# Preparing the output weights of a hybrid attention and recurrence block: half beside the input projection, half beside attention's own projection

## The chip, the core and the metric

The kernel runs on one core of a Trainium2 chip. A core has a matrix engine (TensorE, PE in the profile; its weight loads are PEld), a vector engine (VectorE, DVE), an engine for functions and copies (ScalarE, ACT), a general engine (GpSimd, POOL) and one that only issues transfers (SyncE, SP). Each runs its own instructions in order and waits for the others on semaphores. Transfers between HBM, the large memory, and SBUF, the memory on the chip, are issued by SP, ACT or POOL and carried out by 16 DMA engines. Matmuls write into PSUM, eight banks of 512 float columns.

The metric is the time of one execution in microseconds (us) of device time. A profile is one execution with a record of every instruction: its span runs from the first instruction to the last.

## The reference

One layer of a decoder on a sequence of 1024 tokens of width 1024, in float32. The input is normalised and modulated by a condition `c`, one wide projection makes the inputs of two branches (attention with a window of 128 and a learned sink for each head; a gated linear recurrence), both branches are projected, merged by sigmoid gates, projected again, scaled by a gate made of `c`, added to the input and normalised.

```python
mod = c @ w_ada[l] + b_ada[l]
shift, scale, gate = jnp.split(mod, 3, axis=-1)
h = rmsnorm(x, norm_g[l]) * (1.0 + scale[:, None, :]) + shift[:, None, :]
proj = h @ w_in[l]
q, k, v, g_attn, xr, g_rnn, m_attn, m_rnn = jnp.split(proj, SPLIT_POINTS, axis=-1)
...
denom = jnp.sum(p, axis=-1, keepdims=True) + jnp.exp(sink - m)
...
merged = (jax.nn.sigmoid(m_attn) * (y_attn @ w_attn_proj[l])
          + jax.nn.sigmoid(m_rnn) * (y_rnn @ w_rnn_proj[l]))
x = x + gate[:, None, :] * (merged @ w_out[l])
...
return rmsnorm(x, final_g)
```

Two things of it matter here. `gate * (merged @ w_out)` is computed as `merged @ (w_out * gate)`: the gate row is made from `w_ada`, and the columns of `w_out` are multiplied by it once. And the sinks, 16 numbers, take part in every maximum of attention's scores.

## The kernel before

**Numbers.** A float32 operand is used as a sum of two reduced-precision parts, a high part (`wh`, `hh`, `nh`, ...: a cast on ACT) and the remainder (`wl`, `hl`, `nl`, ...: a subtraction on DVE). Each product is three matmuls: high by high, low by high, high by low. `cast` (L103) and `rest` (L109, and L111 where the weights are scaled) make the two parts of a weight tile.

**The order of the stages.** First the input is normalised and turned, and the first columns are projected (to about 91 us). Then comes the main part of the input projection, on TensorE lines L708 and L1021 (to about 597 us); attention runs from 567 to 745 us amid the end of the projection and the recurrence's projection (`rp_steps`, L171); then attention's projection (`ap_k`, L171, to 838.5 us); then the output projection (`gemm`, L1853) with the last normalisation. Up to L1747 the order on all engines is the program's own (`manual_schedule`); from there to L1924 a planner of the compiler orders the instructions of every engine; from L1925 (`last`) PE, ACT and DVE are again in the program's order.

**The input projection.** `pairs` lists 23 pairs of column chunks. A pair is seven products of 12 matmuls each (a scheme that needs seven products of half-size blocks in place of eight, with sums of weight blocks made by DVE in `tsum`, L730). One product is a slot of about 2.75 us; there are 161 products, numbered by `W["slot"]` in `run`. The first of a product's matmuls needs the high part of its weights, the second the low part, which is made one slot ahead. Beside the products there are four sorts of work on ACT and DVE: what a slot must do (`fixed`), the recurrence's steps (`waiting[0]`, `waiting[1]`), its gate products (`extra`, L1021, 5.5 us each), and work that is due only at the very end (`idle`).

**How `idle` is paced.** `Load.pe`, `Load.act` and `Load.dve` are a running estimate of when each engine will be through with what it has been given. After each slot, `background` first gives out the recurrence's steps as far as the estimate of ACT or DVE does not exceed the end of the slot by more than 2.8 or 2.2 us, then up to four entries of `idle`, as far as it does not exceed it by `slack`. `slack` is 1.0 up to slot 55, then 1.3, or -1.0 while both lists of the recurrence hold work. An entry of `idle` is a list of steps, or a condition that must hold before the next is given out (`slots(n)`: n slots later).

**What is in `idle`.** `w_out_gate` (L1183): eight tiles of `w_gate` (128 x 1024) are loaded by SP into two buffers `wr`, scaled on DVE by their value of `c` and summed in `gate_bc` (L1195, L1198); the sum over the partitions is a product with ones (L1221), which leaves the gate row on every partition (L1227). Then `w_out_blocks(k)` (L1238) for k = 0 to 3: two tiles of `w_out` are loaded, multiplied by the gate row on DVE (`scale`, L1248, 128 x 1024), combined by four differences of halves (`diff`, L1257, 128 x 512), and seven results of 128 x 512 are stored to HBM (`wo_d[0]` to `wo_d[6]`). The output projection loads those back (`load_b`, L1762) and splits them (L1768, L1769).

**Attention's start.** `open_attn` (L1275) opens attention's buffers once the recurrence's lists are empty, and issues the first loads: keys and queries on SP (`load_kq`), the sinks and the values on POOL. It is followed by the units `u` = 0 to 31: `scores` (TensorE, L1325), `maxima_a` (ACT copies scores, L1334), `maxima_d` (for the first block of a group a mask on POOL, L1343; then the negated maximum on DVE, L1345), `weights_a` (exponentials on ACT, L1350), and so on, with one product of the projection between the units (`piece`). `sink(u)` (L1310) copies the sinks into the tile over which the maximum runs, on POOL (L1313).

**The end.** The last row of tiles (row 7) is computed in two halves of 256 columns: `add_to` adds to the input on DVE (L1867), `square` sums squares on ACT (L1871), `root` (L1882), then the reciprocal and the scaling. Rows 4 to 6 are finished by `result` (L1884): a reciprocal and a half row on DVE (L1886, L1887), the other half on ACT (L1889), and the store.

Of the kernel before, what the change touches and what calls it, by code (L numbers as in the profile page):

```python
# [22 lines left out]
P = 128  # L23
# [23 lines left out]
XT = 12  # L47
DIAG = 0, 2, 4
KEEP_BUSY = 4
SLACK = 1.0, 1.3, -1.0  # L50
BANKS = (0, 1, 2, 3), (4, 5, 6, 7)


# [1 line left out]
def tile_hybrid_block(ctx, tc, x, pk, rows, posr, posi, c_row, w_ss, w_gate, w_main, w_v,  # L55
# [78 lines left out]
    yl_d = [tc.dram_tile([P, S], F32, name=f"yl_d{c}") for c in range(KC)]  # L134
    sgr_d = [tc.dram_tile([P, S], F32, name=f"sgr_d{c}") for c in range(KC)]
    wo_d = [tc.dram_tile([4, P, HALF], F32, name=f"wo_d{j}") for j in range(7)]
    tr_d = [tc.dram_tile([P, S], F32, name=f"tr_d{c}") for c in range(KC)]


# [441 lines left out]
    ctab = rpp.tile([P, S], F32, name="ctab")  # L581
    stab = rpp.tile([64, S], F32, name="stab")
    G.memset(ctab[64:128, :], 1.0)
    W["mgt"] = const.tile([P, P], U32, name="mgt")
    mf = rpp.tile([P, HALF], F32, tag="rh", name="mf", bufs=2)[:, :P]
    G.memset(mf, 1.0)
# [68 lines left out]
    fixed = {}  # L655
    waiting = [], []
    idle = []

    def background(d):
# [12 lines left out]
        slack = SLACK[0 if W["slot"] < 56 else 2 if all(waiting) else 1]  # L672
        for _ in range(4 if W["slot"] > 6 else 0):
            while idle and callable(idle[0]) and idle[0]():
                idle.pop(0)
            if not idle or callable(idle[0]):
                break
            a, v = (sum(st_[k] for st_ in idle[0]) for k in (1, 2))
            if (a and max(Load.act, Load.pe) + a > Load.pe + d + slack) or (
                    v and max(Load.dve, Load.pe) + v > Load.pe + d + slack):  # L680
                break
            for st_ in idle.pop(0):
                put(st_)
# [416 lines left out]
    def decay():  # L1100
# [38 lines left out]
            G.tensor_tensor(out=sp8[:], in0=p_, in1=w, op=ALU.add)  # L1139

        load()
        for step in ([("A", 1.5, 0, lam_a)], [("D", 0, 0.2, lam_0)], [("N", 0, 0, lam_1)],
                     [("D", 0, 0.75, reset)]):
            waiting[0].extend([slots(3), step])
# [38 lines left out]
    def w_out_gate():  # L1183
# [4 lines left out]
                t[k] = raw_w(w_gate[k * P:(k + 1) * P, :])  # L1188
            return [("S", 0, 0, f)]

        def step(k):
            def f():
                c = pcol(PK_C, k)
                if k == 0:
                    V.tensor_scalar(out=gate_bc[:], in0=t.pop(k), scalar1=c, scalar2=None,  # L1195
                                    op0=ALU.mult)
                else:
                    V.scalar_tensor_tensor(out=gate_bc[:], in0=t.pop(k), scalar=c,  # L1198
                                           in1=gate_bc[:], op0=ALU.mult, op1=ALU.add)
            return [("D", 0, 1.28 if k else 0.7, f)]  # L1200

        def split_a():
            one = raw_w(rows[0:1, 0:D].to_broadcast([P, D]))
# [21 lines left out]
        def add():  # L1225
            for hf in range(2):
                V.tensor_tensor(out=gate_bc[:, SL[hf]], in0=t["ps"][hf], in1=t["b"][:, SL[hf]],  # L1227
                                op=ALU.add)

        idle.extend([load(0), load(1), slots(3)])  # L1230
        for k in range(KC):
            idle.append(step(k))
            if k + 2 < KC:
                idle.append(load(k + 2))
        idle.extend([[("A", 1.5, 0, split_a)], slots(1), [("D", 0, 1.38, split_d)], slots(2),
                     [("N", 0, 0, product_)], slots(1), [("D", 0, 1.38, add)]])

    def w_out_blocks(k):  # L1238
        t = {}

        def load(i):
            def f():
                t[i] = raw_w(w_out[(k + 4 * i) * P:(k + 4 * i + 1) * P, :])
            return [("S", 0, 0, f)]

        def scale(i):
            def f():
                V.scalar_tensor_tensor(out=t[i], in0=t[i], scalar=0.25, in1=gate_bc[:],  # L1248
                                       op0=ALU.mult, op1=ALU.mult)
            return [("D", 0, 1.28, f)]  # L1250

        def at(n):
            return t[n // 2][:, SL[n % 2]]

        def diff(o, a, b):
            def f():
                V.tensor_tensor(out=at(o), in0=at(a), in1=at(b), op=ALU.subtract)  # L1257
# [8 lines left out]
        idle.extend([load(0), load(1), slots(3), scale(0), scale(1), slots(1),  # L1266
                     store((3, 5), (0, 0), (2, 1)), diff(1, 1, 0), slots(1), store((1, 3)),
                     slots(2), diff(3, 3, 1), diff(0, 3, 0), slots(1), store((3, 2), (0, 4)),
                     diff(2, 2, 3), slots(1), store((2, 6)), slots(2)])
# [5 lines left out]
    def open_attn():  # L1275
        nonlocal at, psx
        psm_ctx.close()
        psx = pool(psx_ctx, "psx", space=PSUM)
        W["kq"] = pool(at_ctx, "kq", bufs=2, side="right")
        W["yo"] = pool(at_ctx, "yo", side="right")  # L1280
        W["pp"] = pool(at_ctx, "pp", bufs=3, side="right")
        at = pool(at_ctx, "at", side="right")
        load_kq(0)
        W["sink"] = W["pp"].tile([P, NH], F32, name="sink", bufs=1)
        dma(W["sink"][:], rows[0:1, 2048:2048 + NH].to_broadcast([P, NH]), G)
        load_v(0)
        load_kq(1)

# [353 lines left out]
        v_prep(g)  # L1642
    decay()
    w_out_gate()
    for k in range(4):
        w_out_blocks(k)
    steps = run(pairs, extra)
    for _ in range(7 * (len(pairs) - N_ATT) - 4):
        next(steps)
# [123 lines left out]
    def ap_k(ps, c, kcs):  # L1773
        for kc in kcs:
            mm_k([ps[:, t] for t in SL], (O[KC + c, 0], O.get((KC + c, 1))), kc, xh=ahh, xl=alh)

    LEFT, RIGHT = SL
    A11 = [(hh[k][0], hl[k][0]) for k in range(4)]
    A12, A22, raw = [], [], []
# [6 lines left out]
    for c in range(KC):  # L1786
# [28 lines left out]
        else:  # L1815
# [134 lines left out]
    V.scalar_tensor_tensor(out=f[:, 0:1], in0=f[:, 1:2], scalar=1.0 / D, in1=f[:, 0:1],  # L1950
# [6 lines left out]
    V.reciprocal(f[:, 3:4], f[:, 2:3])  # L1957
    A.activation(xo[7][:, RIGHT], xo[7][:, RIGHT], AF.Copy, scale=f[:, 3:4])
    V.tensor_scalar(out=xg, in0=xg, scalar1=f[:, 3:4], scalar2=None, op0=ALU.mult)
    dma(out[7 * P:, LEFT], xg)  # L1960
    dma(out[7 * P:, RIGHT], xo[7][:, RIGHT], A)
    last.close()


# [75 lines left out]
```

## Time and profile before

| | us |
|---|---|
| median of 3 runs | 924.14 (924.06 to 925.28) |
| the profiled execution | 924.29 |
| its span | 922.6 |
| TensorE busy | 907.1 |
| VectorE busy | 718.0 |
| ScalarE busy | 566.1 |
| GpSimd busy | 129.3 |

The granted clock of TensorE has a mean of 0.997 over the span. 121.34 MB are read from HBM and 58.95 MB written.

How to read the lines of the profile: in a timeline a row has start, duration, engine, line, operation, output<-inputs, shape and count; a bracket is the time that the engine sat idle before it and what ended that. A matmul's record is longer than its place in the stream, since matmuls overlap; the distance between two starts is the place. "Busy" of TensorE therefore says that it had work in hand, not that it ran at its pace. In a table by stage each engine has its busy time and, in parentheses, its instructions. In the chain of work that ended last a row has start, duration, engine, tile, line and count.

### The profile page before, as it was taken

Reading aid. Unit: us, or ns where it says so; the run is one execution under the profiler, and the core shown is the slowest. Engines: PE = TensorE matmul, PEld = TensorE weight load, DVE = VectorE, ACT = ScalarE, POOL = GpSimd, SP = SyncE. Lnnn points to the kernel's source line nnn. Section 1 sums busy time; section 2 is a strip of 40 time slices with the busy share of each in tenths; the row PEclk is TensorE's granted clock in tenths of the full one; section 3 lists DMA queues with packets and bytes.
Section 4 is the critical chain, followed back from the end, with each engine's and each line's share of the span. In section 5 each row is a group of like instructions: output and inputs, shape, how many; then the busy total and the mean of one; then the engine's idle time right before and its main releaser. Section 6 shows DMA issues by size and latency. Waiting matters only on the chain.

```text
span 922.6 us, 12602 instructions
## 1 busy us (share of the span) xinstructions
PE 907.1 (98%) x4259; PEld 746.4 (81%) x4259; DVE 718.0 (78%) x1071; ACT 566.1 (61%) x1102; POOL 129.3 (14%) x224
## 2 busy tenths in 40 slices
PE   8999999999999999999999999999999999999996
PEld 6789888788888788878888887888888888888885
DVE  6997687878669865887798696899999946678755
ACT  7956554654566855776495874788788733115435
POOL 7420341200000000000000001253444400000000
PEclk9999999999999999999999999999999999999999
DMA  9828589762435453353545357996666279416504
GB/s 362 319 84 274 169 271 302 235 223 92 148 126 198 131 194 122 126 180 131 162 151 204 103 187 257 305 384 231 196 212 206 89 284 376 137 46 228 206 1 182
DMA packets 87204, 180.72 MB, mean 196 GB/s; under 512 B 8626, under 2 KB 29122, under 8 KB 87140
## 3 DMA queue, kind: packets, MB, share of 16 engines
q1 hardware_dynamic: 83056, 167.07, 51.7%
q0 software_dynamic: 3936, 12.59, 4.5%
q8 instruction: 33, 0.54, 0.2%
q14 instruction: 31, 0.25, 0.1%
q10 hardware_dynamic: 148, 0.27, 0.1%
HBM read 121.34 MB, written 58.95 MB: 195 GB/s over the span
## 4 chain that ended last, share of the span: by engine, by line
PE 82%; DVE 9%; ACT 3%; issue 3%; DMA 1%; POOL 1%; DVEq 0%; ACTq 0%; POOLq 0%
PE bk L708 40%; PE rp L171 13%; PE out L1853 6%; PE pgate L1021 5%; PE pmain L171 5%; PE s_ps L1325 3%; PE pv L1398 2%; PE pmain L483 2%; PE bk L483 2%; PE pt L1364 1%; DVE wl L109 1%; PE pmain L1574 1%; PE pmain L1573 1%; PE pmain L1575 1%; DVE ws L730 1%
## 5 line engine op out<-in xcount | busy, mean ns | idle before, releaser
L708 PE MATMUL bk<-nh,wl 128*128 128x512 f32 x368 | 144.5, 393 | 2.9 <-DVE wl L109 2.9
L708 PE MATMUL bk<-nh,wh 128*128 128x512 f32 x368 | 145.5, 395 | 0.0
L708 PE MATMUL bk<-nl,wh 128*128 128x512 f32 x368 | 144.8, 394 | 0.0
L109 DVE TENSOR_TENSOR wl<-r,wh 128x512 fp32r<-128x512 f32 x109 | 79.1, 732 | 9.0 <-ACT wh L103 8.9
L708 PEld LDWEIGHTS bk<-nh,wl 128*128 128x128 f32 x368 | 69.5, 189 | 19.7 <-DVE wl L109 4.5
L103 ACT CAST wh<-r 128x512 fp32r<-128x512 f32 x107 | 65.6, 618 | 32.1 <-PE rp L171 11.0
L708 PEld LDWEIGHTS bk<-nl,wh 128*128 128x128 f32 x368 | 69.4, 189 | 15.8
L708 PEld LDWEIGHTS bk<-nh,wh 128*128 128x128 f32 x368 | 69.6, 189 | 14.4
L708 PE MATMUL bk<-hh,wh 128*128 128x512 f32 x184 | 72.4, 394 | 0.0
L708 PE MATMUL bk<-hh,wl 128*128 128x512 f32 x184 | 72.0, 391 | 0.3 <-DVE wl L109 0.3
L708 PE MATMUL bk<-hl,wh 128*128 128x512 f32 x184 | 72.0, 391 | 0.0
L109 DVE TENSOR_TENSOR wl<-ws,wh 128x512 fp32r<-128x512 f32 x76 | 51.9, 684 | 4.2 <-ACT wh L103 4.2
L1350 ACT ACTIVATE p<-p,small 128x129 f32<-128x129 f32 x128 | 50.1, 400 | 0.5 <-DVE small L1345 0.5
L103 ACT CAST wh<-ws 128x512 fp32r<-128x512 f32 x76 | 46.0, 615 | 3.3 <-PE bk L708 2.2
L708 PEld LDWEIGHTS bk<-hh,wl 128*128 128x128 f32 x184 | 34.6, 188 | 8.4 <-DVE wl L109 1.0
L708 PEld LDWEIGHTS bk<-hl,wh 128*128 128x128 f32 x184 | 34.6, 188 | 7.9
L708 PEld LDWEIGHTS bk<-hh,wh 128*128 128x128 f32 x184 | 34.6, 188 | 7.2
L1325 PE MATMUL s_ps<-ks,qs 128*128 128x256 f32 (+1 forms) x256 | 37.7, 289 | 0.1
L708 PE MATMUL bk<-hha,wl 128*128 128x512 f32 x92 | 36.2, 393 | 1.5 <-DVE wl L109 0.9
L821 ACT ACTIVATE c<-bk 128x512 f32<-128x512 f32 x29 | 17.3, 596 | 32.8 <-PE bk L708 32.8
L886 POOL MEMSET xr<- 128x3 f32 x8 | 0.8, 100 | 260.3 <-PE pgate L1021 235.3
L708 PE MATMUL bk<-hha,wh 128*128 128x512 f32 x92 | 36.2, 394 | 0.0
(376 smaller groups left out, 2325.1 us busy)
## 6 DMA issues: line engine op xcount, KB each, us to landing
r<-w_main SPq DMA_DIRECT2D x100, 256.0 KB, 4.3
wada<-w_ss SPq DMA_DIRECT2D x16, 512.0 KB, 8.9
qs<-q_d SPq DMA_DIRECT2D x16, 512.0 KB, 5.2
wo_d<-wr SPq DMA_DIRECT2D x28, 256.0 KB, 2.8
wo<-wo_d SPq DMA_DIRECT2D x14, 512.0 KB, 5.0
ks<-k_d SPq DMA_DIRECT2D x12, 384.0 KB, 4.5
xt<-x SPq DMA_DIRECT2D x8, 512.0 KB, 6.8
sma_d<-c SPq DMA_DIRECT2D x16, 256.0 KB, 4.5
```

The source lines that it names most:

```text
L103: A.copy(dst[0][:], src)
L109: V.tensor_tensor(out=dst[1][:], in0=src, in1=f32(dst[0][:]), op=ALU.subtract)
L171: mm = T.matmul(ps[hf], ww, xx[kc][hf], start=(kc == 0 and ww is w_h and xx is xh), stop=(kc == KC - 1 and xx is xl))
L483: T.matmul(starts[c][hf], ww[:, c0:c0 + P], xh[kc][hf], start=(kc == 0 and t_ == "h"), stop=(kc == KC - 1 and t_ == "l"))
L708: W["pe"] = T.matmul(ps, ww[:, c], b[kc][xx_], start=(first and kc == 0 and i == 0), stop=(kc == 3 and i == 2), skip_group_check=not first)
L730: V.tensor_tensor(out=R[dst], in0=R[a], in1=R[b], op=op)
L821: A.activation(t["t"], s(), AF.Tanh, scale=0.5)
L1021: W["pe"] = T.matmul(ps[:, SL[hf]], ww[:, c0:c0 + P], xx_[:, SL[hf]], start=(ic == 0 and i == 0), stop=(ic == 1 and i == 2))
L1325: W["pe"] = T.matmul(o, qs[:, j, qc], ks[:, kb:n % 2 + 2, b, :], start=(b == 0), stop=(b == 1))
L1350: A.activation(px[:, j, :], px[:, j, :], AF.Exp, bias=sm[:, 0, j:j + 1], accum_out=sm[:, 1, j:j + 1])
L1398: W["pe"] = T.matmul(pv[:], b, m[:].rearrange("p j q -> p (j q)"), start=(i == 0), stop=(i == len(prods) - 1))
L1853: T.matmul(o, a[k][x_][:, p * P:(p + 1) * P], b[k][y_][:, cols], start=(first and k == 0 and i == 0), stop=(k == 3 and i == 2), skip_group ...
```

## The change

It has four parts.

1. **Pacing.** `slack` no longer depends on the slot and on the recurrence's lists. It is computed from how far the list is behind an even spread over 120 slots from slot 7: 0.3 plus 3.0 times the lateness, held between -0.5 and 0.8. The steps of the gate row and the scaling of the blocks are given out in halves of 512 columns.
2. **Half the blocks move.** Only blocks 0 and 1 are prepared in `idle`. Blocks 2 and 3 are prepared in attention's projection, beside its chunks c = 0 and 1, in the part that the planner orders. For this the gate row is stored to HBM at the end of `w_out_gate` (`gate_d`) and loaded onto all partitions again; the tiles share the buffers `wr` of `load_b`.
3. **The sinks** are loaded at the start of the main projection, in `decay`, into a tile that stays.
4. **The last row.** `result(6)` comes after row 7's last add, square and root; in row 7's scaling the first multiplication of the second half is joined with the second, ACT's half goes to DVE, and the two stores swap their queues.

```diff
-SLACK = 1.0, 1.3, -1.0
+SLACK = 0.3, 3.0, -0.5, 0.8
+SPREAD = 120
+AHEAD = 2
+GROUPS = 4
...
-        slack = SLACK[0 if W["slot"] < 56 else 2 if all(waiting) else 1]
-        for _ in range(4 if W["slot"] > 6 else 0):
+        if W["slot"] == 0:
+            W["idle"] = len(idle)
+        late = (W["slot"] - 7) / SPREAD + len(idle) / max(W["idle"], 1) - 1.0
+        slack = min(max(SLACK[0] + SLACK[1] * late, SLACK[2]), SLACK[3])
+        for _ in range(GROUPS if W["slot"] > 6 else 0):
...
         load()
+        dma(W["sink"][:], rows[0:1, 2048:2048 + NH].to_broadcast([P, NH]), G)
...
-        def step(k):
+        def step(k, hf):
             def f():
-                c = pcol(PK_C, k)
+                c, o, w = pcol(PK_C, k), gate_bc[:, SL[hf]], t[k][:, SL[hf]]
...
-                    V.scalar_tensor_tensor(out=gate_bc[:], in0=t.pop(k), scalar=c,
-                                           in1=gate_bc[:], op0=ALU.mult, op1=ALU.add)
-            return [("D", 0, 1.28 if k else 0.7, f)]
+                    V.scalar_tensor_tensor(out=o, in0=w, scalar=c, in1=o, op0=ALU.mult,
+                                           op1=ALU.add)
+            return [("D", 0, 0.69 if k else 0.4, f)]
...
+            dma(gate_d, gate_bc[0:1, :])
...
-            idle.append(step(k))
+            idle.extend([step(k, 0), step(k, 1)])
...
-        def scale(i):
+        def scale(n):
             def f():
-                V.scalar_tensor_tensor(out=t[i], in0=t[i], scalar=0.25, in1=gate_bc[:],
-                                       op0=ALU.mult, op1=ALU.mult)
-            return [("D", 0, 1.28, f)]
+                V.scalar_tensor_tensor(out=at(n), in0=at(n), scalar=0.25,
+                                       in1=gate_bc[:, SL[n % 2]], op0=ALU.mult, op1=ALU.mult)
+            return [("D", 0, 0.69, f)]
...
-        W["sink"] = W["pp"].tile([P, NH], F32, name="sink", bufs=1)
-        dma(W["sink"][:], rows[0:1, 2048:2048 + NH].to_broadcast([P, NH]), G)
...
-    for k in range(4):
-        w_out_blocks(k)
+    for k in range(AHEAD):
+        idle.extend(w_out_blocks(k, raw_w, gate_bc))
...
+    def raw_t(src):
+        t = tpool.tile([P, D], F32, tag="wr", name="wo_raw", bufs=2)
+        dma(t[:], src)
+        return t[:]
+
+    if AHEAD < 4:
+        gate_ap = tpool.tile([P, D], F32, tag="M", name="gate_bc", bufs=4)
+        dma(gate_ap[:], gate_d.to_broadcast([P, D]))
...
+        if c < 4 - AHEAD:
+            now([st_ for group in w_out_blocks(AHEAD + c, raw_t, gate_ap) if isinstance(group, list)
+                 for st_ in group])
...
-    result(6, RIGHT, LEFT)
...
     root(7)
-    V.tensor_tensor(out=xg[:, c2], in0=xo[7][:, c2], in1=fg_bc[:, c2], op=ALU.mult)
-    V.reciprocal(f[:, 3:4], f[:, 2:3])
-    A.activation(xo[7][:, RIGHT], xo[7][:, RIGHT], AF.Copy, scale=f[:, 3:4])
-    V.tensor_scalar(out=xg, in0=xg, scalar1=f[:, 3:4], scalar2=None, op0=ALU.mult)
-    dma(out[7 * P:, LEFT], xg)
-    dma(out[7 * P:, RIGHT], xo[7][:, RIGHT], A)
+    result(6, RIGHT, LEFT)
+    r = f[:, 3:4]
+    V.reciprocal(r, f[:, 2:3])
+    V.scalar_tensor_tensor(out=xg[:, c2], in0=xo[7][:, c2], scalar=r, in1=fg_bc[:, c2],
+                           op0=ALU.mult, op1=ALU.mult)
+    V.tensor_scalar(out=xg[:, c1], in0=xg[:, c1], scalar1=r, scalar2=None, op0=ALU.mult)
+    dma(out[7 * P:, LEFT], xg, A)
+    V.tensor_scalar(out=xo[7][:, RIGHT], in0=xo[7][:, RIGHT], scalar1=r, scalar2=None,
+                    op0=ALU.mult)
+    dma(out[7 * P:, RIGHT], xo[7][:, RIGHT])
```

More of the change, by code (lines that the diff above doesn't have):

```diff
@@ L136, in tile_hybrid_block @@
     wo_d = [tc.dram_tile([4, P, HALF], F32, name=f"wo_d{j}") for j in range(7)]
+    gate_d = tc.dram_tile([1, D], F32, name="gate_d")
     tr_d = [tc.dram_tile([P, S], F32, name=f"tr_d{c}") for c in range(KC)]
@@ L583, in tile_hybrid_block @@
     G.memset(ctab[64:128, :], 1.0)
+    W["sink"] = const.tile([P, NH], F32, name="sink")
     W["mgt"] = const.tile([P, P], U32, name="mgt")
@@ L657, in tile_hybrid_block @@
     idle = []
+    W["idle"] = 0
     def background(d):
@@ L1189, in load @@
             return [("S", 0, 0, f)]
-        def step(k):
+        def step(k, hf):
             def f():
-                c = pcol(PK_C, k)
+                c, o, w = pcol(PK_C, k), gate_bc[:, SL[hf]], t[k][:, SL[hf]]
                 if k == 0:
-                    V.tensor_scalar(out=gate_bc[:], in0=t.pop(k), scalar1=c, scalar2=None,
-                                    op0=ALU.mult)
-                else:
-                    V.scalar_tensor_tensor(out=gate_bc[:], in0=t.pop(k), scalar=c,
-                                           in1=gate_bc[:], op0=ALU.mult, op1=ALU.add)
-            return [("D", 0, 1.28 if k else 0.7, f)]
+                    V.tensor_scalar(out=o, in0=w, scalar1=c, scalar2=None, op0=ALU.mult)
+                else:
+                    V.scalar_tensor_tensor(out=o, in0=w, scalar=c, in1=o, op0=ALU.mult,
+                                           op1=ALU.add)
+            return [("D", 0, 0.69 if k else 0.4, f)]
         def split_a():
@@ L1236, in w_out_gate, with w_out_blocks @@
                      [("N", 0, 0, product_)], slots(1), [("D", 0, 1.38, add)]])
-    def w_out_blocks(k):
+    def w_out_blocks(k, raw_w, gate_bc):
         t = {}
@@ L1264, in store @@
             return [("S", 0, 0, f)]
-        idle.extend([load(0), load(1), slots(3), scale(0), scale(1), slots(1),
+        return ([load(0), load(1), slots(3), scale(0), scale(1), scale(2), scale(3), slots(1),
                      store((3, 5), (0, 0), (2, 1)), diff(1, 1, 0), slots(1), store((1, 3)),
```

## The prediction

> **What bounds the kernel now.** I read the page's head first, then the busy time by stage, then the timeline of TensorE wherever that table shows it idle.
>
> ```profile
> span 922.6 us, 12602 instructions
> PE 907.1 (98%) x4259; PEld 746.4 (81%) x4259; DVE 718.0 (78%) x1071; ACT 566.1 (61%) x1102; POOL 129.3 (14%) x224
> ```
>
> TensorE (PE) is busy for 907.1 of 922.6 us. The change takes no matmul away, so all that it can win lies in the other 15.5 us and in matmuls that run slowly. A busy share cannot show the second, so the pace is needed: in the chain of work that ended last one undisturbed stretch is
>
> ```profile
> 443.91 63.17 PE bk L708 x276
> ```
>
> 63.17 / 276 = 0.229 us for a 512-column matmul. Any start-to-start time above that is loss. By stage (PE, weight load, DVE, ACT, POOL busy; then clock, DMA share, GB/s):
>
> ```profile
> 277.00:334.00 57.00, 56.21 (x245) 45.40 (x244) 49.47 (x63) 38.57 (x55) 0.00 (x0) 1.00 0.51 180
> 571.00:579.00 8.00, 5.84 (x23) 4.57 (x22) 5.22 (x9) 3.23 (x11) 1.05 (x4) 0.79 0.88 282
> 744.00:838.50 94.50, 94.50 (x414) 77.41 (x413) 58.91 (x68) 24.56 (x37) 0.43 (x1) 1.00 0.60 216
> ```
>
> The largest hole by far is 571 to 579 us, where attention begins; there the granted clock is 0.79 as well. Attention's projection (744 to 838.5) has no hole: what is moved there can only lose.
>
> **The hole where attention begins.** TensorE's timeline, then POOL, ACT and DVE around it:
>
> ```profile
> 572.18 0.40 PE L708 MATMUL bk<-nh,wh 128*128 128x512 f32 x1
> 574.74 0.62 PE L708 MATMUL bk<-nh,wl 128*128 128x512 f32 x1 [2.16 <-DVE wl L109]
> ...
> 578.49 0.39 PE L708 MATMUL bk<-nh,wl 128*128 128x512 f32 x1
> ```
>
> ```profile
> 563.32 0.55 POOL L62 DMA_DIRECT2D sink<-rows  x1
> 571.98 0.19 POOL L1313 COPY p<-sink 128x4 f32<-128x4 f32 x1 [7.05 <-DMA sink<-rows]
> 572.12 0.64 POOL L1343 TENSOR_SCALAR_AFFINE_SELECT p<-p 128x512 f32<-128x512 f32 x1
> 568.57 0.59 ACT L1334 COPY p<-s_ps 128x512 f32<-128x512 f32 x1 [3.07 <-PE s_ps L1325]
> 572.79 0.69 DVE L1345 TENSOR_REDUCE small<-p 128x4 f32<-128x516 f32 x1 [6.71 <-POOL p L1343]
> 574.00 0.69 DVE L109 TENSOR_TENSOR wl<-ws,wh 128x512 fp32r<-128x512 f32 x1
> ```
>
> The sinks are requested at 563.32 and are there 8.6 us later. Everything stands in one file behind them: POOL's copy, its mask, DVE's maximum (idle 6.71 us), and behind the maximum a weight remainder `wl` that has nothing to do with attention but that TensorE needs. Two losses follow. The start of the second matmul is 574.74 - 572.18 - 0.229 = 2.33 us late. Then nine matmuls, from 574.74 to 578.49, take 3.75 us where nine take 2.06: 1.69 us more, the half clock. Together **4.0 us**.
>
> The Trainium skill, "TensorE: Matmul & The Clock Gate", section "Why this matters for your kernels", asks for no idle gap over about 3 us. By it a gap of 2.33 us would cost only itself, and this hole would be worth 2.3 us. The rows disagree: a gap of 2.16 us was followed at once by nine slow matmuls, so the rows decide.
>
> **The change part by part.**
>
> *Sinks loaded early.* One DMA of 8 KB and one issue (0.55 us of POOL) move from 563.3 to the start of the projection, where POOL sits idle anyway; the wait of 7.05 us goes. What is late next? ACT's copy of the first scores ends at 569.16; mask and maximum behind it (0.67 us from 572.12 to 572.79) put the maximum at about 569.9. The remainder started 1.21 us after the maximum and lasts 0.69, so it is ready at 571.8. TensorE wants it at 572.18 + 0.23 = 572.4, so 0.6 us is left. Later remainders have about as much: I followed two more units by the same durations and found 0.5 to 1 us. Value -4.0 us; bounds -2.3 (a new gap below 2 us takes the clock's share back) and -4.0.
>
> *Slower, evenly spread preparation in the projection.* The other holes of the projection:
>
> ```profile
> 166.21 0.40 PE L708 MATMUL bk<-hha,wh 128*128 128x512 f32 x1
> 167.17 0.51 PE L708 MATMUL bk<-hha,wl 128*128 128x512 f32 x1 [0.56 <-DVE wl L111]
> 405.06 0.50 PE L708 MATMUL bk<-hha,wl 128*128 128x512 f32 x1 [0.95 <-DVE wl L109]
> 156.00 1.28 DVE L1198 SCALAR_TENSOR_TENSOR gate_bc<-wr,pk_t,gate_bc 128x1024 f32<-128x1024 f32 x1 [1.84 <-DMA wr<-w_gate]
> L1198 DVE SCALAR_TENSOR_TENSOR gate_bc<-wr,pk_t,gate_bc x7: 1270/1279/1284, 138.7 to 163.3; 128x1024 f32<-128x1024 f32 x7
> 151.22 4.68 DMA wr<-w_gate
> ```
>
> Only the first has preparation in front of it: seven steps of 1.28 us from 138.7 to 163.3, one of them waiting 1.84 us for its load with the weight remainders queued behind it. The new rule starts at slack 0.3 instead of 1.0 and falls as it gets ahead. The list has 74 entries (32 for the gate row, 21 for each of two blocks) over 120 slots: 0.62 an entry a slot, a row of `w_gate` every five slots or 13 us, against 4.7 us for a load (last row). Half-width steps let a remainder in after 0.6 us, not 1.2. So I take this hole as closed: 167.17 - 166.21 - 0.23 = 0.73, and 0.11 of the next start: **-0.8 us**. Bounds 0 and -0.8.
>
> The hole at 405.1, the one in 277 to 334 (0.79 us by its stage's row) and their neighbours, 3.1 us in all, stand in recurrence work, and the old rule kept preparation out of there:
>
> ```profile
> 275.72 0.69 DVE L1257 TENSOR_TENSOR wr<-wr 128x512 f32<-128x512 f32 x1
> ...
> 333.62 1.41 DVE L1257 TENSOR_TENSOR wr<-wr 128x512 f32<-128x512 f32 x2
> L1248 DVE SCALAR_TENSOR_TENSOR wr<-wr,gate_bc x8: 1218/1218/1221, 205.8 to 512.3; 128x1024 f32<-128x1024 f32 x8
> L1257 DVE TENSOR_TENSOR wr<-wr x16: 681/685/692, 215.9 to 565.4; 128x512 f32<-128x512 f32 x16
> ```
>
> Under the new rule about nine half-width steps fall into 277 to 334 and 350 to 415 (36 slots at 0.62, two fifths of the entries being DVE work). The rule admits a step only while the modelled backlog of DVE stays under 2.75 + 0.8 us, and the recurrence itself may fill it to 2.75 + 2.8, so the steps take free places. Value 0; bounds +5.4 (all nine, 0.6 us each, in front of an awaited remainder) and -3.1 (these holes go too, as the order is dealt anew).
>
> *Two blocks moved into attention's projection.* By the last two rows half of 9.7 + 11.0 us leaves the projection: 10.4 us of DVE, with 4 loads of 512 KB, 14 stores of 256 KB, and one new load of the gate row to all partitions (512 KB), 6 MB in all. DVE has 94.5 - 58.9 = 35.6 us free there. The queues pass these on the way (SP's in order, so a store that waits for DVE holds back the weights behind it):
>
> ```profile
> 760.00:770.00 10.00, 10.00 (x45) 8.22 (x44) 4.43 (x5) 4.14 (x6) 0.00 (x0) 1.00 1.04 401
> 763.00 2.06 ACT L103 CAST wh<-r 128x512 fp32r<-128x512 f32 x3 [0.79 <-DMA r<-w_ap]
> 763.65 2.13 DVE L109 TENSOR_TENSOR wl<-r,wh 128x512 fp32r<-128x512 f32 x3 [0.18 <-ACT wh L103]
> 772.37 0.62 PE L171 MATMUL rp<-ah,wh 128*128 128x512 f32 x2
> ```
>
> The next chunk's weights are done at 765.8 and used from 772.4: 6.6 us of margin, and each later chunk has 11 us. The early loads of the finished output weights that stand there now cannot come so early any more and make room for the new ones. The DMA engines are full there (share 1.04, 401 GB/s); 1.5 MB ahead of the weights delays them 4 us, inside the margin. The first output weights are needed at 838.5, some 40 us after block 3 can be stored. Value 0; bounds 0 and +4.2 (one gap of 2.5 us and the half clock behind it).
>
> *The last row's adds first.* DVE and the stores at the end:
>
> ```profile
> 915.44 0.19 ACT L1871 ACTIVATION_READ_ACCUMULATOR jk<-xo 128x1 f32 x1
> 916.27 0.33 SPq L62 DMA_DIRECT2D out<-xo  x1
> 916.46 0.15 DVE L1950 SCALAR_TENSOR_TENSOR fs<-fs 128x1 f32<-128x1 f32 x1
> 916.53 0.41 DVE L1867 TENSOR_TENSOR xo<-xo,out 128x256 f32<-128x256 f32 x1
> 917.91 0.16 DVE L1957 RECIPROCAL fs<-fs 128x1 f32<-128x1 f32 x1 [0.50 <-ACT fs L1882]
> 918.11 0.49 DVE L1959 TENSOR_SCALAR xg<-xg,fs 128x512 f32<-128x512 f32 x1
> 918.86 0.38 ACTq L62 DMA_DIRECT2D out<-xo  x1
> GB/s 0 0 0 0 0 0 174 397 422 397 397 422 422 397 149 0 0 0 0 0 62 285 397 397 397 373 372 397 385 112 0 0 0 0 0 0 0 0 0 0
> ```
>
> The tiny step can start when the accumulator is read, 915.63; the add follows at 915.8 instead of 916.5, and the reciprocal at 917.2. Then DVE does three steps in a row (0.41 as the add of 256 columns, half of 0.49, 0.49), where ACT and DVE shared them: the last store goes at 918.5, 0.4 us sooner. But row 6 now waits behind: its ACT half follows the last root (917.1, and 0.75 as from 918.11 to the issue at 918.86), so its 512 KB go at 917.9 instead of 916.27. The last row (40 slices of 0.165 us from 916) shows that stores alone already run at about 400 GB/s. 1.05 MB at 390 GB/s are 2.7 us, from 918.7 to 921.4, where packets ended at about 920.9: **+0.5 us**; bounds -0.4 (the sooner issue is kept) and +0.7. The Trainium skill, "DMA: Bandwidth & Descriptors", section "Specifications", puts the ceiling at 435 GB/s; an estimate by it: these stores would need 2.4 us, and the end would lose 0.2.
>
> **Sum.** -4.0 - 0.8 + 0 + 0.5 = -4.3 us. The profiled execution took 924.29 us (1.7 outside its span), the median of three is 924.14: 924.14 - 4.3 = **919.8 us**.
>
> **Rivals.**
> - *The recurrence's holes close as well*: up to -3.1 more, 916.7 us. For it: 10 us less DVE work before attention; against: these holes had no preparation in front. 0.14.
> - *Another wait takes the place of the sinks.* The first scores need `qs`:
>
> ```profile
> 560.98 0.60 SPq L62 DMA_DIRECT2D qs<-q_d  x1
> 567.49 1.05 PE L1325 MATMUL s_ps<-ks,qs 128*128 128x128 f32 x8
> qs<-q_d SPq DMA_DIRECT2D x1, 512.0 KB, 6.3
> ```
>
>  It landed at 567.3, 0.2 us before use. If the recurrence ends one slot later, it is issued 2.75 us later: a gap of 2.5 us and 1.7 for the clock, 924.0 us. Against: no preparation's stores are left in front of that issue. 0.10.
> - *The moved blocks hold up attention's projection* by one such gap, 4.2 us: 924.0 us. 0.06.
> - *The slow clock is not the gap's doing* and stays where the gap goes: 919.8 + 1.7 = 921.5 us. The nine slow matmuls right behind the gap speak against it. 0.04. (It is what the skill's clock page, named above, would make of a gap this short.)
> - *Slower: preparation in the recurrence's windows.* The nine steps land in front of awaited remainders, 5.4 us, and one gap grows past 2 us, 1.7 more: 919.8 + 7.1 = 926.9 us. It decides from 4.3 + 1.85 = 6.2 us of new gaps. For it: DVE is busy for 49.5 of 57 us there. 0.07.
>
> **How the numbers follow.** The forecast has 0.59. 0.2% (1.85 us) is about what a measurement of this kernel tells from no change, so faster means below 922.3 us. Forecast, first and fourth rival, and the mild forms of the second and third (0.03) give 0.80; the rest of these two 0.13; the last 0.07. The range reaches down to the first rival, 916.6, and up to 922.8, which takes in the forecast's bounds (the tail's +0.7, no gain at 167 us, 2 us of a small new gap).
>
> **What would show it.** Right: POOL's copy from `sink` at the first scores waits for no DMA; clock 1.00 from 565 to 580; no idle time over 1 us before an L708 matmul there; no hole near 166; TensorE full through attention's projection; row 6's store issued 1.5 us closer to the end and the time from the last matmul to the end half a us longer. Wrong: an idle row of TensorE before `s_ps` with `qs` or `ks` as its cause, new idle rows before L708 between 277 and 415, or one before L171 or L1853.

## The result, and the profile after

The changed kernel took **926.92 us** (median of 7 runs, 926.37 to 927.82) where the kernel before took 924.14: a ratio of 1.0028, 95% interval 1.0017 to 1.004. It is slower by 0.28% or 2.6 us; forecast were 4.3 us the other way, and the range ended at 922.8.

The head of the changed kernel's page:

```profile
span 925.3 us, 12617 instructions
PE 913.4 (99%) x4259; PEld 746.8 (81%) x4259; DVE 720.0 (78%) x1088; ACT 566.5 (61%) x1100; POOL 129.5 (14%) x224
```

The number of matmuls is the same, 4259. But TensorE's busy time rose from 907.1 to 913.4 us while the span grew by 2.7. So its idle time did shrink, by 3.6 us, and the matmuls themselves became longer. The change adds no matmul and alters none.

Busy time by stage of the changed kernel (columns as in the prediction: stretch, PE, weight load, DVE, ACT, POOL; clock, DMA share, GB/s). The second and third row answer to rows of the prediction:

```profile
420.00:550.00 130.00, 130.00 (x559) 104.65 (x558) 95.57 (x123) 88.13 (x120) 0.20 (x2) 1.00 0.39 129
571.00:579.00 8.00, 8.00 (x44) 6.81 (x44) 3.25 (x6) 3.08 (x9) 0.91 (x3) 1.00 0.49 138
744.00:838.50 94.50, 94.50 (x409) 76.47 (x408) 67.55 (x84) 22.65 (x35) 1.16 (x2) 1.00 0.78 281
855.00:905.00 50.00, 50.00 (x220) 41.04 (x219) 33.89 (x57) 23.02 (x44) 0.00 (x0) 1.00 0.29 106
```

And two of these stretches in the kernel before:

```profile
420.00:550.00 130.00, 130.00 (x569) 106.47 (x568) 103.19 (x133) 91.97 (x126) 0.20 (x2) 1.00 0.43 145
855.00:905.00 50.00, 50.00 (x220) 41.00 (x219) 32.32 (x57) 21.60 (x43) 0.00 (x0) 1.00 0.30 109
```

Read 571 to 579 first: 8.00 of 8 us busy and clock 1.00, where it was 5.84 and 0.79. The hole is gone, as forecast. Then read 420 to 550. TensorE is full in both kernels, the clock is 1.00 in both, and still 559 matmuls fit where 569 did. Ten matmuls are 2.3 us lost in 130 us, with no idle row and no clock row that shows it. Attention's projection is alike: 409 for 414. In the output stage (855 to 905) both kernels do 220: there the pace is unchanged. The chain of waits has the same in one row (start, duration, line, count), to be set beside the row of 63.17 us in the prediction:

```profile
446.88 64.40 PE bk L717 x276
```

64.40 / 276 = 0.2333 us a matmul, 4.5 ns more than before.

TensorE and POOL where attention begins, in the changed kernel:

```profile
572.23 0.39 PE L717 MATMUL bk<-nh,wl 128*128 128x512 f32 x1
572.46 0.40 PE L717 MATMUL bk<-nl,wh 128*128 128x512 f32 x1
572.69 1.00 PE L1333 MATMUL s_ps<-ks,qs 128*128 128x128 f32 x8
573.53 0.45 PE L717 MATMUL bk<-nh,wh 128*128 128x512 f32 x1
573.82 0.39 PE L717 MATMUL bk<-nh,wl 128*128 128x512 f32 x1
```

```profile
566.99 0.51 POOL L1321 COPY p<-sink 128x4 f32<-128x4 f32 x1
```

POOL's copy of the sinks waits for no DMA and is done 5 us before the first scores, and no matmul has an idle time in front.

So nearly every sign that the prediction named for "right" is there, and none of those named for "wrong". Three came smaller than named: near 166 us the hole is not gone but shorter and sooner (0.38 us idle before 160.8, where it was 0.56 before 167.2; VectorE's steps of the gate row stand ahead of it as they did), row 6's store stands 1.1 us closer to the end and not 1.5, and the time from the last matmul to the end grew by 0.3 us and not 0.5.

```profile
158.69 1.41 DVE L1207 SCALAR_TENSOR_TENSOR gate_bc<-wr,pk_t,gate_bc 128x512 f32<-128x512 f32 x2 [3.31 <-DMA wr<-w_gate]
160.77 0.51 PE L717 MATMUL bk<-hh,wl 128*128 128x512 f32 x1 [0.38 <-DVE wl L114]
```

The loss is one that it had no sign for.

### The profile page after: what moved, and what is told of

It is laid out like the page before. It is cut to its first block, busy times and chain, and to the rows that moved or that the text cites. A ratio compares the mean times of both kernels' runs of the same rounds, so it can differ in the third digit from the quotient of the medians.

```text
span 925.3 us, 12617 instructions
## 1 busy us (share of the span) xinstructions
PE 913.4 (99%) x4259; PEld 746.8 (81%) x4259; DVE 720.0 (78%) x1088; ACT 566.5 (61%) x1100; POOL 129.5 (14%) x224
## 4 chain that ended last, share of the span: by engine, by line
PE 91%; DVE 5%; ACT 2%; DMA 1%; issue 1%; DVEq 0%; ACTq 0%
PE bk L717 47%; PE rp L175 13%; PE out L1872 6%; PE pgate L1030 5%; PE pmain L175 5%; PE s_ps L1333 3%; PE pv L1406 3%; PE pmain L487 2%; PE bk L487 2%; PE pt L1372 1%; PE pmain L1583 1%; PE pmain L1582 1%; PE pmain L1581 1%; ACT jk L1890 1%; DMA wr<-w_gate 1%
## 5 line engine op out<-in xcount | busy, mean ns | idle before, releaser
L717 PE MATMUL bk<-hla,wh 128*128 128x512 f32 x92 | 36.3, 395 | 0.0
```

The lines of the kernel that those rows point to most:

```text
L717: W["pe"] = T.matmul(ps, ww[:, c], b[kc][xx_], start=(first and kc == 0 and i == 0), stop=(kc == 3 and i == 2), skip_group_check=not first)
```

## The experiments

**Two theories.** Theory A: the sinks' new tile does it by its place alone. It is 64 bytes per partition in `const`, the first pool on the left of SBUF. Left pools are stacked upward, so the streamed operands (`hh`, `hl`, `nh`, `nl`) stand 64 bytes further on; the pool of weights (`wh`, `wl`) stands on the right and doesn't move. In the program's list of tiles `hh4` goes from 24,096 to 24,160, and `wh` stays at 208,864. Theory B: the new order of the preparation slows the matmuls, by the instructions that run beside them.

All kernels below that aren't said to change the order issue the same instructions on each engine in the same order as the kernel they start from. Every ratio is to runs of the kernel before on the same chip and beside it; its median there was 922.7 us for e1 to e8 and 924.1 for e9 to e16, so times of different sets are compared by their ratios.

### First four: the tile alone

```diff
# e1 (16 floats), e4 (8 floats): the kernel before
+    const.tile([P, 16], F32, name="pad")
     W["mgt"] = const.tile([P, P], U32, name="mgt")
# e2: the changed kernel
     W["sink"] = const.tile([P, NH], F32, name="sink")
+    const.tile([P, 16], F32, name="pad")
# e3: the kernel before
+    W["sink"] = const.tile([P, NH], F32, name="sink")
+    const.tile([P, 16], F32, name="pad")
...
         load()
+        dma(W["sink"][:], rows[0:1, 2048:2048 + NH].to_broadcast([P, NH]), G)
...
-        W["sink"] = W["pp"].tile([P, NH], F32, name="sink", bufs=1)
-        dma(W["sink"][:], rows[0:1, 2048:2048 + NH].to_broadcast([P, NH]), G)
```

> The kernel before with an unused tile of 64 bytes per partition in the first pool, so that every tile behind it on that side of SBUF stands 64 bytes further on, as in the changed kernel; nothing else differs, TensorE's order is the same. Theory A (the new place of the tiles slows the matmuls): the pace of the projection's matmuls goes from 0.229 to 0.233 us as in the changed kernel; 1920 of them x 4.0 ns = 7.7 us and some 400 in attention's projection x 3.3 ns = 1.3 us, of which the holes at 317, 395 and 404 us (3.1 us) may swallow a part: 930 us (928 to 933.5). Theory B (the new order of the preparation slows the matmuls): 924.1 us and a pace of 0.229.

Measured: 930.57 us, ratio 1.0089 (1.0068 to 1.011), so 8.2 us lost by a tile that nothing uses. Its row of the chain of waits:

```profile
448.47 64.40 PE bk L708 x276
```

64.40 us for 276 matmuls, to the hundredth what the changed kernel takes. Theory B has nothing that could do this. Whether anything is left for it beside theory A is settled by e5 below.

> The kernel before with an unused tile of 32 bytes in the first pool: the left tiles start at 64 modulo 128 where they started at 32 (96 with 64 bytes). Under theory A this is a third point of the rule: if only the place of the weights' (96) and the moving tiles' being equal modulo 128 is slow, 924.1 us; if every place other than 32 is, as the gates' matmuls of the kernel before hint (230 ns at 32, 234 at 64, 231.5 at 96), 930 to 934 us. Theory B: 924.1 us.

Measured: 931.83 us, ratio 1.0097 (1.0073 to 1.0121); the same row has 64.41:

```profile
449.63 64.41 PE bk L708 x276
```

> The changed kernel with 64 unused bytes behind the sinks' tile, so that the later tiles stand 128 bytes further on than in the kernel before, not 64; nothing else differs. Theory A, with only the place within 128 bytes deciding: the pace is back at 0.229 us and the time at 926.9 - 9.0 = 917.9 us, or up to 920 if holes come back as TensorE gets faster. Theory B: 926.9 us and a pace of 0.233. If a 128-byte step slows as well, the pace stays at 0.233 here and A holds in e1 only.

Measured: 927.49 us, ratio 1.005 (1.0034 to 1.0067). The guess that only the place within 128 bytes counts was wrong. The chain's longest undisturbed row:

```profile
361.74 58.80 PE bk L717 x252
```

58.80 / 252 = 0.2333.

> The kernel before with the sinks loaded early alone, and the later tiles 128 bytes further on (64 for the sinks, 64 unused). The prediction's first step gives 924.1 - 4.0 = 920.1 us (bounds 920.1 to 921.8), the hole at 572 us and the half clock gone, holes at 166 and 277 to 415 us as before. Theory A and B agree here unless 128 bytes slow the matmuls as well: then about 926.

Measured: 930.32 us, ratio 1.0079 (1.006 to 1.0098). The row:

```profile
448.94 64.39 PE bk L710 x276
```

The expected 920.1 us was missed for the reason of e2: 128 bytes slow the matmuls like 64.

Three shifts, of 32, 64 and 128 bytes, all slow; only the kernel before is fast. One stage is the same in all: the output stage, whose two operands both stand on the left and so move together. That made a new form of theory A: not the place of a tile decides, but the **distance** from the streamed tile's start to the weights' start. It is 24,096 - 208,864 = 64 modulo 256 (and 512) in the kernel before, 128 in the changed one, 96 in e4, 192 in e2 and e3.

### Next four: the distance

```diff
# e5: the changed kernel; sink_t is the first tile of the pool of weights
+    sink_t = wp.tile([P, NH], F32, name="sink")
-    W["sink"] = const.tile([P, NH], F32, name="sink")
+    W["sink"] = sink_t
# e6: e3 with the same sink_t in place of its two new tiles
# e7: the kernel before
+    const.tile([P, 48], F32, name="pad")
# e8: the changed kernel
-    pk_t = const.tile([P, PK_N], F32, name="pk_t")
+    pk_t = wp.tile([P, PK_N], F32, name="pk_t")
...
     W["sink"] = const.tile([P, NH], F32, name="sink")
+    const.tile([P, 64], F32, name="pad")
```

> The changed kernel with the sinks' tile as the first of the right-hand pool of weights, which opens 64 bytes lower for it: the left tiles and the weights' tiles stand at the addresses of the kernel before (their distance is 64 modulo 512 again), and every engine issues the same instructions in the same order as in the changed kernel. Theory A in its new form (the distance from a moving tile's start to the start of the weights, modulo 512 or 256, sets the pace: 64 gave 229 ns, 96, 128 and 192 gave 233): pace 229 ns, and the time is what the prediction's steps give without the tile's side effect, 4.3 us below the kernel before, 7.4 if the recurrence's holes stay closed as they are in the changed kernel. Theory B (the new order slows the matmuls): 0.28% above the kernel before, and 233 ns.

Measured: **917.11 us, ratio 0.9942** (0.9929 to 0.9954). The row is back at the 63.17 us of the kernel before:

```profile
440.38 63.17 PE bk L717 x276
```

This is the whole change, instruction for instruction, with one tile of 64 bytes in another place: 5.4 us faster than the kernel before instead of 2.6 slower.

> The kernel before with the sinks' early load alone, their tile again the first of the right-hand pool, so that left tiles and weights stand as in the kernel before. Theory A: the prediction's first step alone, 4.0 us below the kernel before (bounds 2.3 and 4.0), pace 229 ns, the holes between 277 and 415 us still there. Theory B: the same, as the order of the preparation is the old one. With the run before it this splits the change: whatever that one has more than 4.0 us is the preparation's and the tail's.

Measured: 919.76 us, ratio 0.9967 (0.9956 to 0.9979), so -3.0 us (-1.9 to -4.1); the span is 918.5 us, 4.1 below the one before. The first scores of this kernel now wait for their queries:

```profile
568.25 1.08 PE L1323 MATMUL s_ps<-ks,qs 128*128 128x128 f32 x8 [0.41 <-DMA qs<-q_d]
```

That is the prediction's second rival, with 0.41 us in place of 2.5.

> The kernel before with 192 unused bytes in the first pool: distance 256 modulo 512. If the pace goes by the distance modulo 256, 256 is like 0, which the output stage has for 220 of its matmuls (226.8 ns): 2350 matmuls x 2.3 ns = 5.4 us below the kernel before. If it goes by 512, 256 is one more shifted place like 96, 128 and 192: 7 to 9 us above the kernel before. Theory B: no difference.

Measured: 917.85 us, ratio 0.9946 (0.9932 to 0.9959): 5.0 us below the kernel before, by unused bytes alone.

```profile
441.85 62.61 PE bk L708 x276
```

62.61 / 276 = 0.2268 us. Distance 256 is like 0, the distance of most matmuls of the output stage, so the period is 256.

> The changed kernel with the constants' tile of 384 bytes moved to the bottom of the right-hand pool and 256 unused bytes behind the sinks: the left tiles' distance to the weights is 0 modulo 512, the order of all instructions is that of the changed kernel. Theory A: the pace of the output stage's matmuls at distance 0, 226.8 ns, in the projections too: 2350 x (233.0 - 226.8) = 14.6 us below the changed kernel, about 912.5 us where that takes 926.9, unless the remainders on VectorE are then late. Theory B: as the changed kernel.

Measured: 911.74 us, ratio 0.9888 (0.9873 to 0.9903).

```profile
437.65 62.61 PE bk L717 x276
```

The expected 14.6 us below the changed kernel were worked out from the pace alone; by the ratios (1.0028 - 0.9888) it is 12.9 us.

### Which operand, and the parts of the change

```diff
# e9: the changed kernel; the pad stands above the weights' tiles
+    wp.tile([P, 32], F32, name="pad")
# e10: e5 with
-AHEAD = 2
+AHEAD = 4
# e11: e5 with the last row's lines of the kernel before
# e12: e5 with
-SLACK = 0.3, 3.0, -0.5, 0.8
+SLACK = 1.0, 1.3, -1.0
...
-        late = (W["slot"] - 7) / SPREAD + len(idle) / max(W["idle"], 1) - 1.0
-        slack = min(max(SLACK[0] + SLACK[1] * late, SLACK[2]), SLACK[3])
+        slack = SLACK[0 if W["slot"] < 56 else 2 if all(waiting) else 1]
```

> The changed kernel with 128 unused bytes above the weights' tiles: all right-hand tiles stand 128 bytes lower, the left ones stay where the changed kernel has them, and the order of all instructions is the changed kernel's. Distance 256 modulo 512. If the distance between the two operands decides, the pace is 227 ns and the time that of the run at distance 0, 1.1% below the kernel before. If it is the place of the left tiles alone, nothing has changed for them: 233 ns and 0.3% above the kernel before.

Measured: 912.08 us, ratio 0.9876 (0.9856 to 0.9895).

```profile
437.76 62.61 PE bk L717 x276
```

The left tiles stand where the slow changed kernel has them; moving the weights by 128 bytes brings 227 ns. It is the distance.

One stage of one kernel shows it too. By the program's list, the output stage's matmuls with `hha` and `hla` have distance 0, and 96 of those with `s` have distance 128, in every kernel here. In the changed kernel 48 of each sort stand side by side:

```profile
884.63 0.62 PE L1872 MATMUL out<-wo,hha 128*128 128x512 f32 x2
...
895.52 11.32 PE L1872 MATMUL out<-wo,s 128*128 128x512 f32 x48
906.68 0.62 PE L1872 MATMUL out<-wo,mh 128*128 128x512 f32 x2
```

The first 48 take 226.9 ns each (884.63 to 895.52), those with `s` 232.5 (895.52 to 906.68).

> The changed kernel with the sinks' tile on the right (distance 64) and AHEAD = 4: all four blocks stay in the input projection under the new pacing, none goes to attention's projection. The prediction's third step costs the moving at 0 in attention's projection. If it was the fewer steps that closed the recurrence's holes, they come back here, 1 to 3 us above the run with two blocks moved (0.9942 of the kernel before); if it was the pacing and the half-width steps, the same time as that run within 0.5 us.

Measured: 923.93 us, ratio 0.9998 (0.9986 to 1.001), 5.2 us above e5 and more than was expected either way. Of the recurrence's holes the one at 317 us stays closed, but those at 394 and 402 us are back:

```profile
403.28 0.51 PE L717 MATMUL bk<-hha,wl 128*128 128x512 f32 x1 [0.95 <-DVE wl L112]
```

Beyond them there is a new place, in attention, and it costs more than they do. The first load of `yh` in SyncE's queue of e5, then SyncE's queue and TensorE's timeline of e10:

```profile
587.70 0.42 SPq L65 DMA_DIRECT2D yh<-yh_d  x1
```

```profile
592.31 6.95 SPq L65 DMA_DIRECT2D wo_d<-wr  x3
599.32 0.52 SPq L65 DMA_DIRECT2D yh<-yh_d  x1
599.93 0.64 SPq L65 DMA_DIRECT2D yl<-yl_d  x1
```

```profile
605.57 0.73 PE L175 MATMUL rp<-yl,wh 128*128 128x512 f32 x2 [0.25 <-DMA yl<-yl_d]
606.87 0.72 PE L175 MATMUL rp<-yh,wh 128*128 128x512 f32 x2 [0.58 <-DMA yh<-yh_d]
610.07 1.22 PE L175 MATMUL rp<-yl,wh 128*128 128x512 f32 x2 [2.00 <-DMA yl<-yl_d]
611.09 0.63 PE L1406 MATMUL pv<-phc,vd 128*128 128x512 f32 x1
611.52 0.63 PE L1406 MATMUL pv<-plc,vd 128*128 128x512 f32 x1
```

With all four blocks the evenly paced list isn't done when attention begins. Three stores of prepared weights hold the in-order queue for 6.95 us, the loads of `yh` and `yl` come behind them, and TensorE idles three times. After the last gap, of 2.00 us, the matmuls are 0.43 us apart: the half clock. So the moved blocks belong to the pacing: a slow pace needs the shorter list.

> The changed kernel with the sinks' tile on the right (distance 64) and the last row in its old order. The prediction's fourth step says that the new order costs 0.5 us (bounds -0.4 and +0.7): this run is 0.5 us below the one with the new order, seen in the time from the last matmul's start to the end, 7.7 us there and 7.5 in the kernel before. If the new order gains, this run is slower.

Measured: 916.29 us, ratio 0.9919 (0.9899 to 0.9938). The interval overlaps e5's, so the whole time doesn't settle it; the trace does for this stretch. Last matmul and stores of e5:

```profile
907.27 0.28 PE L1872 MATMUL out<-wo,ml 128*128 128x256 f32 x1
...
909.80 1.10 SPq L65 DMA_DIRECT2D out<-xo  x2
...
910.17 0.38 ACTq L65 DMA_DIRECT2D out<-xg  x1
```

and of e11 (row 6 leaves at 908.58, the last row's halves at 910.92 and 911.16; in e5 row 6 leaves at 909.80):

```profile
907.51 0.28 PE L1872 MATMUL out<-wo,ml 128*128 128x256 f32 x1
...
908.58 0.33 SPq L65 DMA_DIRECT2D out<-xo  x1
...
910.92 0.33 SPq L65 DMA_DIRECT2D out<-xg  x1
911.16 0.38 ACTq L65 DMA_DIRECT2D out<-xo  x1
```

From the last matmul's start to the end of the span it is 915.0 - 907.3 = 7.7 us in e5 and 914.8 - 907.5 = 7.3 in e11: the new order costs 0.4 us there.

> The changed kernel with the sinks' tile on the right (distance 64) and the old rule of slack (1.0, 1.3, -1.0 and no pacing) for the half-width steps; two blocks are still moved. If the pacing closed the hole at 166 us as the prediction's second step has it, that hole is back here, +0.8 us; if the fewer and shorter steps did, there is no difference. If the pacing also closed the recurrence's holes, +2.8 us more.

Measured: 920.39 us, ratio 0.9963 (0.995 to 0.9976); 1.9 us above e5 by the ratios, 3.7 by the spans. The recurrence's holes are back, where and as long as the kernel before has them. TensorE in e12:

```profile
316.99 0.40 PE L717 MATMUL bk<-nh,wh 128*128 128x512 f32 x1
318.16 0.50 PE L717 MATMUL bk<-nh,wl 128*128 128x512 f32 x1 [0.78 <-DVE wl L112]
...
405.29 0.50 PE L717 MATMUL bk<-hha,wl 128*128 128x512 f32 x1 [0.95 <-DVE wl L112]
```

VectorE ahead of the first one, in e12 and then in e5:

```profile
314.65 2.28 DVE L1087 TENSOR_TENSOR_SCAN rz<-av,it 128x1024 f32<-128x1024 f32 x1
316.85 0.66 DVE L777 TENSOR_TENSOR c<-bk,p 128x512 f32<-128x512 f32 x1
317.43 0.68 DVE L112 TENSOR_TENSOR wl<-ws,wh 128x512 fp32r<-128x512 f32 x1
```

```profile
305.78 2.28 DVE L1087 TENSOR_TENSOR_SCAN rz<-av,it 128x1024 f32<-128x1024 f32 x1
307.99 1.26 DVE L915 SCALAR_TENSOR_TENSOR xc<-xr,pk_t,xc 128x1024 f32<-128x1024 f32 x1
309.16 0.68 DVE L112 TENSOR_TENSOR wl<-ws,wh 128x512 fp32r<-128x512 f32 x1
```

In e12 the recurrence's scan of 2.28 us stands ahead of an awaited remainder `wl`, with one short step between them. In e5 the same scan is issued 9 us sooner, and no remainder is late behind it. That the pacing moves the scan is shown; by which steps it does so was not followed. For the hole near 166 us the run says little: e12 idles 0.55 us at 186.6, e5 0.40 us at 158.4.

### The best version, and the rest of the rule

e13 is e9 with the last row of the kernel before. e14, e15 and e16 are e1 with 56, 24 and 40 floats.

> The changed kernel with 128 unused bytes above the weights' tiles (distance 256 modulo 512) and the last row in its old order: both findings together. The run at this distance took 0.9876 of the kernel before, and the old order was worth 0.45 us in the trace (7.71 to 7.26 from the last matmul's start to the end): 0.987 of the kernel before, some 911.5 us where that takes 923.5. If the end is hidden by something else at this pace, the same as without the old order.

Measured: 912.08 us, ratio 0.9875 (0.9857 to 0.9893), no different from e9. From the last matmul to the end its trace has 7.3 us for e9's 7.7, but its projection ends 0.6 us later. That the old order is worth anything in the whole isn't shown. e8, e9 and e13 are the best that was found, some 1.2% below the kernel before and 1.5% below the changed one.

> The kernel before with 224 unused bytes in the first pool: distance 288, that is 32 modulo 256. Measured so far: 0 gives 226.7 to 227.1 ns, 64 gives 229, 96, 128 and 192 give 233. If the pace goes by the distance modulo 256 and is good near 0, 32 lies between 227 and 229 ns, and the profiled span some 4 us below that of the kernel before. If only 0 and 64 are good (steps of 64), 233.

> The kernel before with 96 unused bytes in the first pool: distance 160. Between 128 and 192, both 233 ns: 233 ns and a span some 5 us above that of the kernel before. Should it be at 229 or less, the rule is not one of a good stretch from 0 to 64.

> The kernel before with 160 unused bytes in the first pool: distance 224, the last step before 256, where the pace is 227. If the good stretch runs from 0 to 64 alone, 233 ns, as at 192; if it reaches to both sides of 0, 229 or less.

Measured, in one execution each: 932.11, 933.29 and 930.62 us. Their rows of the chain, in this order:

```profile
449.97 64.40 PE bk L708 x276
```

```profile
450.94 64.65 PE bk L708 x276
```

```profile
448.70 64.39 PE bk L708 x276
```

Even 32 bytes off the good place costs the full price. By distance modulo 256, each from 276 matmuls of the projection: 0 gives 226.8 ns, 32 gives 233.3, **64 gives 228.9**, 96 gives 233.4, **128 gives 233.3** (the change), 160 gives 234.2, 192 gives 233.3, 224 gives 233.3. Two places of eight are good, and the kernel before stood on the second best.

## Why the prediction was wrong, step by step

**What failed** is the step that is named "Sinks loaded early". It priced the DMA, its issue and the wait, and not the tile: 64 bytes put under nearly all other tiles of the left side. Behind it stands the pace that the prediction read first, 0.229 us, and then used as a constant of the chip. It was a property of where two tiles stood, and the change moved one of them. What it cost is seen between two kernels of the same instructions, the changed one and e5: 1.0028 - 0.9942 = 0.86% of 924 us, 7.9 us (10.3 by the spans, 925.3 and 915.0, from two sets of runs). From the rows: 2.3 us in 130 us of the projection, over its 475 us from 92 to 567, are 8.4; five matmuls in attention's projection are 1.2 more. With no term for it in the sum, no chance and no bound could hold it: neither the range nor the 0.07 for "slower" contained this mechanism. The rival that ended slower needed holes in the recurrence; these closed. That its 926.9 us is the measured time is chance.

**The sum of the four steps held**, at an unmoved distance. It was put at -4.3 us; e5 gives -5.4 (-4.2 to -6.6) by the ratio, -7.6 by the spans. That it lies so near is in part luck, for the steps miss in opposite directions.

- *Sinks*: forecast -4.0, e6 gave -3.0 by the ratio and -4.1 by the span. Gap and half clock went together; the fourth rival (the slow clock stays) is refuted. The waiting queries of the second rival came, at a sixth of their price.
- *Pacing*: the hole at 166 us was to go for -0.8. It shrank and moved: in e5 a matmul starts 0.56 us late at 158.4, where the kernel before was 0.73 late. The steps are not as even as the prediction took them: in the changed kernel seven come between 150.9 and 161.3 us, and one of them still waits 3.31 us for its load. The recurrence's holes, valued at 0, closed all but 0.3 us, so the first rival, given 0.14, was right about them. What closed them is not one thing: the lighter list alone (e12) closes none, the new pacing alone (e10) closes the one at 317 us, and those at 394 and 402 us needed both. The term was mis-sized; the bound of -3.1 held it.
- *Moved blocks*: forecast 0, and attention's projection stayed full (94.50 of 94.50 us). What the prediction didn't see is what moving them prevents: 5.2 us (e10), the larger part of it where attention begins.
- *Last row*: forecast +0.5 with row 6's store at 917.9; measured +0.3 against e6 and the kernel before (7.7 for 7.4 us), 0.4 against e11. Counted from the last matmul, the store at 920.11 in the changed kernel is at 917.7.

So one missing term of 8 us hid four steps that were good in their sum, one of them, the pacing, mis-sized.

## What to carry to other kernels

A new tile is also a move of every tile that is stacked behind it. Where a kernel is bound by matmuls, count the matmuls in a full stretch of the profile before and after (569 and 559 here), for a busy share of 100% at full clock doesn't show the pace; if the pace has changed, put an unused tile of 32 to 224 bytes on one side and profile it again. And before a change is judged by its time, repeat it with the addresses of the kernel before: the verdict on this one turned round.

## What the runs showed of the hardware

**The distance of the operands.** For 128x512 matmuls of this kernel (fp32r, new weights for each) the time from start to start goes by the distance of the two operands' starts in SBUF, with period 256 bytes: 226.8 ns at 0, 228.9 at 64, 233 to 234 at the other multiples of 32. The granted clock is 1.00 at all of them. Why the distance matters is not settled by any run here. The Trainium skill, "TensorE: Matmul & The Clock Gate", section "Back-to-back issue gap", gives N / 2.4 + 2.5 ns for a matmul by itself, by which an estimate for 512 columns is 216 ns, and about 131 ns at 512 columns for a sustained stream of weight loads and matmuls. It has no term for addresses, and the traces agree with neither figure: no row of 200 such matmuls or more came below 226.7 ns here.

**Short gaps and the clock.** An idle gap of 2.16 us in the kernel before, one of 1.94 us in e7 and one of 2.00 us in e10 (behind two shorter ones) were each followed by the half clock. One of 1.65 us in e14 was not (the clock is 1.00 from 577 to 590 us), nor was one of 0.95 us in e12. The rows of e7 and e14:

```profile
571.41 0.50 PE L708 MATMUL bk<-nh,wl 128*128 128x512 f32 x1 [1.94 <-DVE wl L109]
```

```profile
582.50 0.51 PE L708 MATMUL bk<-nh,wl 128*128 128x512 f32 x1 [1.65 <-DVE wl L109]
```

The length of one gap is not the whole rule: in e2 the clock is 0.52 from 24 to 27.5 us, with no single gap over 1 us in front. The Trainium skill, "TensorE: Matmul & The Clock Gate", section "Why this matters for your kernels", puts the limit at about 3 us of idle time; the three traces with gaps of 1.94 to 2.16 us disagree.
